# Two delta-rule scans in lockstep, link by link, in shared PSUM tiles

## The chip, the cores and the metric

The kernel runs on one core of a Trainium2 chip. The metric is device time in microseconds. TensorE is called PE here (PEld is its weight load), VectorE DVE, ScalarE ACT, GpSimd POOL and SyncE SP.

## The reference

One inference step of a hybrid diffusion backbone, two layers over 640 tokens (512 latent tokens of a sample and 128 of a prompt), model width 1024. Each layer mixes tokens with three groups of heads side by side, gated DeltaNet (gdn, four heads of 64), HGRN2 (hgrn, four heads of 64) and latent attention (mla), and then runs a SwiGLU feed-forward. The part that matters here is the recurrence of gated DeltaNet, over chunks of 64 tokens, forward and backward:

```python
def step(s, xs):
    att_i, u_i, w_i, qd_i, kt_i, gl_i = xs
    v_new = u_i - jnp.einsum('bhck,bhkv->bhcv', w_i, s)
    o = jnp.einsum('bhck,bhkv->bhcv', qd_i, s) + jnp.einsum('bhij,bhjv->bhiv', att_i, v_new)
    s = s * gl_i[..., None, None] + jnp.einsum('bhck,bhcv->bhkv', kt_i, v_new)
    return s, o
...
s_fin, o = lax.scan(step, s0.astype(F32), xs)
```

HGRN2's recurrence is chunked too; within a chunk its attention matrix is built from pairwise decays.

## The kernel before, in words

All 640 tokens are processed together: activations lie as (128 features, 640 tokens). The large projections (`gemm`, matmuls on line L656) take each weight block of 128x512 from memory, split it into two reduced-precision parts (`wh` on ACT, L632, and `wl` on DVE, L633) and multiply by the two parts of the activation, each matmul 128x128 by 128x320. These matmuls fill most of PE's time.

The heads of gdn form two pairs (pr 0 and 1), a pair lying on the 128 partitions. For a pair, `gdn_raw` makes queries, keys and values from the projection, and `gdn_main` makes the matrices of every chunk: decays, the triangular matrix P, its inverse R (the 16x16 blocks are inverted on DVE by 15 rounds of L866 and L868, with a DMA trip through memory before and after; then transposes from L885, and matmuls from L896 to L921), and at its end it runs the scan. The scan has ten links: eight of the sample and two of the prompt, which alternate at first. A link handles a forward and a backward chunk: ks = K S (four 64x64 fp32 matmuls, L946), r = v - g ks (two DVE operations, L949), xx = R r (four matmuls, L954), vt and VN (two DVE operations, L957 and L958), ds = K^T vt (four matmuls, L964), and the new state S (two DVE operations, L969). Every step needs the one before.

`mix_out` (L985) forms the pair's output afterwards. `hgrn_main` does the same for a pair of hgrn heads: a prelude of exponentials and logarithms over (128, 2, 640) from Abs (L1012) on, then six levels of `merge` (matmuls on L1040, 64x64, with masked copies on L1044), each level needing products on DVE (L1076) and copies on ACT (L1065) between them, and then state matmuls (L1089). `mla_proj` (matmuls on L1208 and L1209) and the attention (from L1276) follow.

What runs beside what comes from a list, one entry a group of chains that take turns, `|` between chains, `+` within a chain, `*2` two turns at a time:

```python
ORDER = "g0 g1 i0|2*e0 i1+L0|2*m0+e1 P0|f0 a0|m1+f1"
```

g is gdn (raw and main), e gdn's output, i hgrn's projection, m hgrn_main, f hgrn's output, L and P the projections of mla, a the attention; the digit is the pair. The program is written in that order, and the framework's scheduler then orders each engine's instructions with a cost model, by priority and program order, and places them as data and buffers allow. So an instruction that waits for data is passed by later ones, such as the large matmuls of the next projection. `use` sets the pools from which blocks and PSUM tiles are taken: a pair's blocks come from `w0` or `w1` (seven buffers each), its small PSUM tiles from `c0` or `c1`. g0, e0, m0 use `w0`; g1, e1, m1 use `w1`, and m0 takes blocks that gdn's pair 0 leaves.

Of the kernel before, what the change touches and what calls it, by code (L numbers as in the profile page):

```python
# [12 lines left out]
ALU = mybir.AluOpType  # L13
# [8 lines left out]
NC = NT // 64  # L22
# [15 lines left out]
HP = (slice(0, 64), slice(64, 128))  # L38
# [121 lines left out]
def two(ap, i0, i1):  # L160
    st = i1 - i0
    if st > 0:
        return ap[:, i0:i1 + 1:st]
    return ap[:, i0:(i1 - 1 if i1 > 0 else None):st]


class Builder:
# [634 lines left out]
    def gdn_main(self, l, pr, KQ, VT):  # L802
        nc = self.nc
        u0 = pr * 2
        flat = lambda ap: ap.rearrange("p d c t -> p (d c t)")
        beta, btail, egl, ngc, g = (ap[:, u0:u0 + 2] for ap in (self.beta, self.btail, self.egl, self.ngc, self.g))
# [6 lines left out]
        for gi in range(3):  # L813
            for which, dst in ((0, E), (1, EG)):
                t = self.ps()
                for i, gu in enumerate(gU):
                    st, sp = i == 0, i == 1
                    if gi < 2:
                        r = gu[:, gi, 0:NCS].rearrange("p c t -> p (c t)")
# [3 lines left out]
                if gi == 2 and which == 0:  # L823
                    for d in range(2):
                        for i, gu in enumerate(gU):
                            nc.tensor.matmul(t[:, d * 128:d * 128 + 128], lhsT=self.LmR[:, d],
                                             rhs=gu[:, d, NCS:].rearrange("p c t -> p (c t)"), start=i == 0, stop=i == 1)
# [4 lines left out]
        for c0 in range(0, NC, 4):  # L832
            n = min(4, NC - c0)
# [8 lines left out]
        att = E  # L842
# [3 lines left out]
        for gp in range(8):  # L846
            b = gp % 4
            nc.sync.dma_start(out=drP[gp].rearrange("u j i -> j u i"),
                              in_=P[gp * 16:gp * 16 + 16].rearrange("p d c t -> p (d c) t")[:, :, b * 16:b * 16 + 16])
# [13 lines left out]
        for j in range(15):  # L863
# [3 lines left out]
                                    in1=W[:, :, j:j + 1, 0:j + 1].to_broadcast(sh), op=ALU.mult)  # L867
# [3 lines left out]
        for gp in range(8):  # L871
            b = gp % 4
            nc.sync.dma_start(out=X[gp * 16:gp * 16 + 16].rearrange("p d c t -> p (d c) t")[:, :, b * 16:b * 16 + 16],
                              in_=drT[gp].rearrange("u j i -> j u i"))
        nc.vector.tensor_tensor(out=EG, in0=EG, in1=KQ[:, 1].unsqueeze(1).to_broadcast([128, 2, NC, 64]), op=ALU.mult)
        K_, V = KQ[:, 1], VT[:, 0].rearrange("p (c t) -> p c t", t=64)
        self.token_major([lambda i: KQ[:, 0, 2 * i:2 * i + 2].rearrange("p c t -> p (c t)"), lambda i: VT[:, 0, i * 128:i * 128 + 128]], [K_, V])
        QD = EG
# [26 lines left out]
        R = self.blk([128, 2, NC, 64])  # L905
# [21 lines left out]
        SH = self.blk([128, 2, NC, 64])  # L927
        VN = self.blk([128, 2, NC, 64])
        fl = lambda ap: ap.rearrange("p d c t -> p (d c) t")
        SHf, VNf = fl(SH), fl(VN)  # L930
        bf = beta.rearrange("p d c -> p (d c)")
        bt = btail.rearrange("p d c -> p (d c)")
        bc2 = lambda ap: ap.unsqueeze(2).to_broadcast([128, 2, 64])
        nc.sync.dma_start(out=two(SHf, 0, NC + NCS - 1), in_=self.I["gst"][l, :, :, pr])
        nc.vector.memset(two(SHf, NCS, 2 * NC - 1), 0.0)
        for step in range(NCS):
            for c0, n in ((0, NCS), (NCS, NC - NCS)):
                if step >= n:
                    continue
                cs = (c0 + step, c0 + n - 1 - step)  # L940
                i0, i1 = cs[0], NC + cs[1]
                last = step == n - 1
                ks = self.ps((128, 2, 64))
                for d in range(2):
                    for h in HP:
                        nc.tensor.matmul(ks[h, d], lhsT=KQ[h, 0, cs[d]], rhs=SH[h, d, cs[d]], start=True, stop=True)  # L946
                r = self.small(f"st_r{pr}", [128, 2, 64], bufs=1)
                for d in range(2):
                    nc.vector.scalar_tensor_tensor(out=r[:, d], in0=ks[:, d], scalar=ngc[:, d, cs[d]:cs[d] + 1], in1=V[:, cs[d]],  # L949
                                                   op0=ALU.mult, op1=ALU.add)  # L950
                xx = self.ps((128, 2, 64))
                for d in range(2):
                    for h in HP:
                        nc.tensor.matmul(xx[h, d], lhsT=R[h, d, cs[d]], rhs=r[h, d], start=True, stop=True)  # L954
                if not (last and c0 == 0):
                    vt = self.small(f"st_v{pr}", [128, 2, 64], bufs=1)
                    nc.vector.tensor_tensor(out=vt, in0=xx, in1=bc2(two(bt, i0, i1)), op=ALU.mult)  # L957
                nc.vector.tensor_tensor(out=two(VNf, i0, i1), in0=xx, in1=bc2(two(bf, i0, i1)), op=ALU.mult)  # L958
                if last and c0 == 0:
                    continue  # L960
                ds = self.ps((128, 2, 64))
                for d in range(2):
                    for h in HP:
                        nc.tensor.matmul(ds[h, d], lhsT=K_[h, cs[d]], rhs=vt[h, d], start=True, stop=True)  # L964
                if last:
                    sto = self.small("stout", [128, 2, 64], bufs=2)
                for d in range(2):
                    dst = sto[:, d] if last else SH[:, d, cs[d] + 1 - 2 * d]
                    nc.vector.scalar_tensor_tensor(out=dst, in0=SH[:, d, cs[d]], scalar=egl[:, d, cs[d]:cs[d] + 1],  # L969
                                                   in1=ds[:, d], op0=ALU.mult, op1=ALU.add)  # L970
                if last:
                    nc.sync.dma_start(out=self.O["gst"][l, :, :, pr], in_=sto)
        return lambda h, c: [(SH[h, d, c], QD[h, d, c]) for d in range(2)] + [(VN[h, d, c], att[h, d, c]) for d in range(2)]

    def mix_out(self, dst, terms):
        nc = self.nc
# [394 lines left out]
    def layer(self, l, h, pre):  # L1371
        nc, I = self.nc, self.I
# [13 lines left out]
                pass  # L1386
        self.use("c0", "w0")
        self.gates(l, inp(W_AB))
        terms, gd, mix, st, mb = [None] * 4, [None] * 2, [None] * 8, [None, None], []

        def gdn(pr):
            self.use(f"c{pr}", f"w{pr}")
            gd[pr] = (rb([128, 2, NC, 64]), rb([128, 2, NT]))
            self.gdn_raw(l, pr, inp, *gd[pr])
            if pr == 0:
                fill(100)
            terms[pr] = self.gdn_main(l, pr, *gd[pr])

        def gdn_end(pr):
            self.use(f"c{pr}", f"w{pr}")  # L1400
# [28 lines left out]
        def hgrn_end(pr):  # L1429
            self.use(f"c{pr}", f"w{pr}")  # L1430
            yield from self.mix_out(hs[pr][0][:, 0], terms[2 + pr])
            mix[2 + pr] = self.finish_mixer(hs[pr][0][:, 0], hs[pr][2], self.vec[:, l, V_HNW:V_HNW + 1], f"w{pr}")

        steps = {"g": gdn, "e": gdn_end, "i": hgrn_in, "m": hgrn, "f": hgrn_end, "L": lambda n: mla_in(), "P": lambda n: mla(),
                 "a": lambda n: self.attention(l, st[1], mix, range(4))}
        for group in ORDER.split():
# [5 lines left out]
        for s in range(2):  # L1442
            tag, bt = f"c{s}", ("w1", "r")[s]
# [24 lines left out]
        last, us = None, []  # L1468
        for i, n in enumerate(range(NSP, NFF)):
# [3 lines left out]
            last = self.seven(l, n, A, us[-1], last, rb([128, 4, HALF]))  # L1473
# [14 lines left out]
        for pieces, ns in (((0, 1), range(4)),) + tuple(((q,), range(4, KD)) for q in (0, 1)):  # L1488
# [13 lines left out]
            tag, bt = f"c{s}", ("h", "w0")[s]  # L1502
# [121 lines left out]
```

## Time and profile before

| | us |
|---|---|
| three runs | 1975.47, 1977.1, 1982.02; median 1977.1 |
| the profiled execution | 1979.4 |
| its span (first to last instruction) | 1977.6 |
| PE busy | 1910.7 (97%) |
| DVE busy | 1370.9 (69%) |
| ACT busy | 997.1 (50%) |
| mean granted PE clock | 0.99 of full |

A row of the profile's groups reads: line, engine, operation, output<-inputs, shapes, count, busy time, mean time of one. Times in the text are microseconds from the span's start. The two layers lie one behind the other; in layer 0 the gdn scans run from 220 to 321, in layer 1 from 1195 to 1300.

### The profile page before, as it was taken

What the parts mean: (1) busy time and instruction counts of PE and PEld (TensorE: products, weight loads), DVE (VectorE), ACT (ScalarE), POOL (GpSimd) and SP (SyncE); (2) the same over time, 40 slices, a digit from 0 to 9 for tenths busy, and PEclk for the clock granted to TensorE, in tenths of its full rate; (3) what the DMA queues carried; (4) which work ended last, traced back from release to release, by engine and by line L of the source; (5) the groups of instructions that cost most, each with busy time, mean ns of one, the idle gap of its engine ahead of it and who ended that gap; (6) DMA issues with size and microseconds to landing.
All of it is one profiled execution on the core that took longest, in us unless ns stands there. A gap on an engine that the chain in (4) does not pass through costs nothing. (4 is left out here: it accounts for less than half of the span.)

```text
span 1977.6 us, 40034 instructions
## 1 busy us (share of the span) xinstructions
PE 1910.7 (97%) x15688; PEld 1739.2 (88%) x15688; DVE 1370.9 (69%) x2962; ACT 997.1 (50%) x2086; POOL 16.2 (1%) x64
## 2 busy tenths in 40 slices
PE   6999999999999999999999999999999999999996
PEld 3748888888999979999998987888899999999996
DVE  5537567696677757788887786678756977776245
ACT  4515253754676435551355551648457755555243
POOL 0000000000000000000000000000000000000000
PEclk9999999999999999999999999999999999999998
DMA  9652211210554452256764232112036532223344
GB/s 320 207 183 64 59 42 28 58 37 18 187 176 150 139 166 85 86 167 202 235 192 133 62 100 52 29 42 58 5 100 187 167 117 86 86 86 103 87 139 141
DMA packets 157486, 226.56 MB, mean 115 GB/s; under 512 B 38769, under 2 KB 65521, under 8 KB 157297
## 3 DMA queue, kind: packets, MB, share of 16 engines
q1 hardware_dynamic: 156656, 222.70, 36.8%
q8 instruction: 123, 2.02, 0.4%
q0 software_dynamic: 640, 1.31, 0.3%
q14 instruction: 67, 0.54, 0.1%
HBM read 209.99 MB, written 12.65 MB: 113 GB/s over the span
## 5 line engine op out<-in xcount | busy, mean ns | idle before, releaser
L632 ACT ACTIVATE wh<-raw 128x512 fp32r<-128x512 f32 (+2 forms) x634 | 391.0, 617 | 603.8 <-PE g L656 413.5
L633 DVE TENSOR_TENSOR wl<-raw,wh 128x512 fp32r<-128x512 f32 (+1 forms) x610 | 408.2, 671 | 303.4 <-ACT wh L632 265.9
L656 PE MATMUL g<-h,wh 128*128 128x320 f32 x2448 | 541.4, 319 | 8.6 <-ACT h L481 3.3
L656 PEld LDWEIGHTS g<-h,wh 128*128 128x128 f32 x2448 | 401.3, 189 | 41.0 <-issue 16.2
L656 PE MATMUL g<-h,wl 128*128 128x320 f32 x1224 | 338.3, 316 | 0.5 <-DVE wl L633 0.5
L656 PE MATMUL g<-w,wh 128*128 128x320 f32 x1152 | 246.1, 314 | 5.5 <-ACT r L1448 5.5
L656 PEld LDWEIGHTS g<-h,wl 128*128 128x128 f32 x1224 | 218.4, 189 | 12.0 <-issue 6.4
L656 PEld LDWEIGHTS g<-w,wh 128*128 128x128 f32 x1152 | 191.0, 191 | 6.2 <-ACT r L1448 6.0
L656 PE MATMUL g<-r,wh 128*128 128x320 f32 x768 | 165.5, 313 | 0.0
L656 PE MATMUL g<-w,wl 128*128 128x320 f32 x480 | 132.7, 314 | 0.0
L563 PE MATMUL g<-h,wh 128*128 128x320 f32 x768 | 129.0, 310 | 0.0
L656 PEld LDWEIGHTS g<-r,wh 128*128 128x128 f32 x768 | 127.5, 190 | 0.6
L563 PEld LDWEIGHTS g<-h,wh 128*128 128x128 f32 x768 | 116.3, 188 | 3.6 <-issue 3.4
L557 DVE TENSOR_TENSOR raw<-raw,raw 128x512 f32<-128x512 f32 x128 | 88.0, 687 | 2.2
L656 PEld LDWEIGHTS g<-w,wl 128*128 128x128 f32 x480 | 87.4, 192 | 0.2
L563 PE MATMUL g<-w,wh 128*128 128x320 f32 x512 | 85.9, 310 | 0.0
L563 PE MATMUL g<-r,wh 128*128 128x320 f32 x512 | 85.5, 309 | 0.0
L299 DVE SCALAR_TENSOR_TENSOR h<-h,silu_c,h 128x512 f32<-128x512 f32 x112 | 78.5, 745 | 4.6 <-DMA h<-in_w_ada_dram 4.5
L563 PEld LDWEIGHTS g<-w,wh 128*128 128x128 f32 x512 | 77.6, 188 | 3.4 <-ACT r L575 3.4
L656 PE MATMUL g<-r,wl 128*128 128x320 f32 x288 | 79.3, 312 | 0.0
L563 PEld LDWEIGHTS g<-r,wh 128*128 128x128 f32 x512 | 77.7, 188 | 0.0
L563 PE MATMUL g<-h,wl 128*128 128x320 f32 x384 | 71.9, 309 | 0.0
(378 smaller groups left out, 3094.8 us busy)
## 6 DMA issues: line engine op xcount, KB each, us to landing
raw<-in_w_ffi_dram SPq DMA_DIRECT2D x224, 256.0 KB
raw<-in_w_ffo_dram SPq DMA_DIRECT2D x120, 256.0 KB
raw<-in_w_in_dram SPq DMA_DIRECT2D x106, 256.0 KB
w<-in_w_ada_dram SPq DMA_DIRECT2D x96, 256.0 KB
raw<-in_w_out_dram SPq DMA_DIRECT2D x64, 256.0 KB
h<-in_w_ada_dram SPq DMA_DIRECT2D x32, 512.0 KB
r<-in_w_ada_dram SPq DMA_DIRECT2D x32, 256.0 KB
r<-in_xT_dram SPq DMA_DIRECT2D x6, 640.0 KB
```

The source lines that it names most:

```text
L299: nc.vector.scalar_tensor_tensor(out=acc[:, s], in0=raw[:, k % 2], scalar=c, in1=acc[:, s], op0=ALU.mult, op1=ALU.add)
L557: nc.vector.tensor_tensor(out=o, in0=a, in1=b, op=ALU.add)
L563: nc.tensor.matmul(ps, lhsT=w[e][:, k], rhs=a[f][:, k], start=first and i == 0, stop=i == 11, skip_group_check=not first)
L632: self.nc.scalar.activation(hi, src, AF.Copy)
L633: self.nc.vector.tensor_tensor(out=lo, in0=src, in1=hi.bitcast(F32), op=ALU.subtract)
L656: self.nc.tensor.matmul(ps[h], lhsT=w[:, k], rhs=rhs(e, kk, h), start=(kk == 0 and i == 0), stop=(kk == nk - 1 and i == 2))
```

## The change

The scan becomes a generator that yields after each of its steps. `gdn_main` returns it instead of running it, and a new function, `gdn_scan`, runs after the matrices of pair 1 are made, and goes through the ten links with both pairs: ks of pair 0 and of pair 1, then r of both, and so on. For each link the two pairs share three PSUM tiles, (128, 2, 2, 64) instead of (128, 2, 64), with one half for each pair, and two small tiles, `st_r` and `st_v`. The number of instructions and their shapes stay. In the changed kernel the scan's lines are L944, L947, L952, L955, L960, L961 and L969, and lines from L985 on lie 12 lower (L985 is L997, L1040 is L1052, L1208 is L1220).

```diff
+        def scan(step, c0, n, both):
...
+            ks, xx, ds = (both[i][:, pr] for i in range(3))
+            r, vt = (both[i][:, pr] for i in (3, 4))
+            for d in range(2):
+                for h in HP:
+                    nc.tensor.matmul(ks[h, d], lhsT=KQ[h, 0, cs[d]], rhs=SH[h, d, cs[d]], start=True, stop=True)
+            yield
...
+        return scan, lambda h, c: [(SH[h, d, c], QD[h, d, c]) for d in range(2)] + [(VN[h, d, c], att[h, d, c]) for d in range(2)]
+
+    def gdn_scan(self, scans):
         for step in range(NCS):
             for c0, n in ((0, NCS), (NCS, NC - NCS)):
                 if step >= n:
                     continue
...
-                ks = self.ps((128, 2, 64))
...
-                r = self.small(f"st_r{pr}", [128, 2, 64], bufs=1)
...
-        return lambda h, c: [(SH[h, d, c], QD[h, d, c]) for d in range(2)] + [(VN[h, d, c], att[h, d, c]) for d in range(2)]
+                both = [self.ps((128, 2, 2, 64), tag) for tag in ("c0", "c1", "c0")]
+                both += [self.small(name, [128, 2, 2, 64], bufs=1) for name in ("st_r", "st_v")]
+                runs = [scan(step, c0, n, both) for scan in scans]
+                while runs:
+                    runs = [r for r in runs if next(r, runs) is not runs]
...
         def gdn(pr):
...
-            terms[pr] = self.gdn_main(l, pr, *gd[pr])
+            scans[pr], terms[pr] = self.gdn_main(l, pr, *gd[pr])
+            if pr == 1:
+                self.gdn_scan(scans)
```

The order of the instructions follows from the scheduler. On DVE, in layer 0, pair 1's block inversion (L866, L868) stands like this before, with the links of pair 0's scan between its rounds (`st_r` and `st_v` are the scan's small tiles, `w` blocks, `m` PSUM tiles):

```order
L866 TENSOR_TENSOR w_258_1893<-w_258_1893,w_257_1892 80x2x48
L868 TENSOR_TENSOR w_257_1892<-w_257_1892,w_258_1893 80x2x12x4
L969 SCALAR_TENSOR_TENSOR w_148_1269<-w_148_1269,eg_592,m_1312 128x64 x2
...
L949 SCALAR_TENSOR_TENSOR st_r_161_1324<-m_1319,eg_592,r_603 128x64 x2
L866 TENSOR_TENSOR w_258_1893<-w_258_1893,w_257_1892 80x2x55
L868 TENSOR_TENSOR w_257_1892<-w_257_1892,w_258_1893 80x2x11x5
L957 TENSOR_TENSOR st_v_163_1332<-m_1327,eg_592 128x128
L958 TENSOR_TENSOR w_149_1270<-m_1327,beta_575 128x2x64
```

and like this after:

```order
L866 TENSOR_TENSOR w_209_1670<-w_209_1670,w_208_1669 80x2x48
L868 TENSOR_TENSOR w_208_1669<-w_208_1669,w_209_1670 80x2x12x4
L866 TENSOR_TENSOR w_209_1670<-w_209_1670,w_208_1669 80x2x55
L868 TENSOR_TENSOR w_208_1669<-w_208_1669,w_209_1670 80x2x11x5
L866 TENSOR_TENSOR w_209_1670<-w_209_1670,w_208_1669 80x2x60
L868 TENSOR_TENSOR w_208_1669<-w_208_1669,w_209_1670 80x2x10x6
```

The scan's operations have moved behind the inversion; on PE, 194 large matmuls (213 in layer 1) stand beside it with only pair 0's first ks ahead of them. On PE, in layer 1, the scan's last third is a run without large matmuls after the change (`r` and `w` are the scan's operands; 66 matmuls in all stand in it):

```order
L960 MATMUL m_13404<-st_v_13406,r_11892 64x64 x4
L960 MATMUL m_13404<-st_v_13406,r_12522 64x64 x4
L944 MATMUL m_13443<-w_1836_12518,r_11892 64x64 x4
L944 MATMUL m_13443<-w_1912_13148,r_12522 64x64 x4
L952 MATMUL m_13444<-st_r_13446,w_1833_12428 64x64 x4
L952 MATMUL m_13444<-st_r_13446,w_1909_13058 64x64 x4
L960 MATMUL m_13445<-st_v_13447,r_11892 64x64 x4
L960 MATMUL m_13445<-st_v_13447,r_12522 64x64 x4
L944 MATMUL m_13484<-w_1836_12518,r_11892 64x64 x4
L944 MATMUL m_13484<-w_1912_13148,r_12522 64x64 x4
```

Before, a link of either pair had large matmuls or merges of m0 between its steps to its end. The merges of m0 stood, in layer 1, on PE like this before (L1040, with scan 1 and large matmuls, `g`, between them):

```order
L1040 MATMUL m_14066<-r_11621,w_2118_14035 64x64
L1040 MATMUL m_14084<-r_11621,w_2118_14035 64x64 x4
L656 MATMUL g_14777<-h_11046,wh_14810 128x320
L656 MATMUL g_14778<-h_11560,wh_14810 128x320
L656 MATMUL g_14777<-h_11048,wh_14810 128x320
L946 MATMUL m_13538<-w_2007_13417,r_12791 64x64 x4
L656 MATMUL g_14778<-h_11562,wh_14810 128x320
...
L964 MATMUL m_13554<-st_v_2038_13551,r_12791 64x64 x4
L656 MATMUL g_14778<-h_11562,wh_14810 128x320
L656 MATMUL g_14777<-h_11046,wl_14811 128x320
L1040 MATMUL m_14161<-w_2112_14006,w_2118_14035 64x64 x3
```

and like this after (L1052; L754 are transposes, L1125 matmuls of a norm):

```order
L1125 MATMUL m_14979<-w_2138_14973,cst 128x320
L1052 MATMUL m_13974<-r_11575,w_2026_13943 64x64 x16
L1052 MATMUL m_13992<-r_11575,w_2026_13943 64x64 x4
L754 MATMUL m_15528<-cst,r_13846 128x128 x4
L754 MATMUL m_15537<-cst,r_13846 128x128
L1052 MATMUL m_14069<-w_2020_13914,w_2026_13943 64x64 x16
L1052 MATMUL m_14087<-w_2020_13914,w_2026_13943 64x64 x4
L1052 MATMUL m_14100<-w_2020_13914,w_2026_13943 64x64 x16
L1052 MATMUL m_14118<-w_2020_13914,w_2026_13943 64x64 x4
L1052 MATMUL m_14195<-w_2020_13914,w_2026_13943 64x64 x16
```

In both layers the merges now stand in one run without large matmuls. Between the last matmul of the scans and the first merge stand 92 large matmuls in layer 0 and 47 in layer 1, with the output matmuls of both pairs. Over the whole program the places where a stretch of large matmuls is broken by other matmuls went from 234 to 219. Outside the stretch from g1 to the attention of each layer PE's order is as before.

## Rows read from the trace of the kernel before

**Rows 1.** The page: busy time, share of the span, instructions.

```profile
PE 1910.7 (97%) x15688; PEld 1739.2 (88%) x15688; DVE 1370.9 (69%) x2962; ACT 997.1 (50%) x2086; POOL 16.2 (1%) x64
```

**Rows 2.** Windows: stretch and length, busy time by engine (instructions), granted clock, DMA.

```profile
220.60:260.00 39.40, 39.37 (x370) 30.85 (x372) 24.36 (x94) 7.00 (x15) 0.00 (x0) 1.00 0.18 49
...
367.40:412.80 45.40, 42.96 (x340) 36.97 (x339) 37.92 (x67) 38.76 (x77) 2.17 (x4) 1.00 0.25 65
...
1256.60:1301.80 45.20, 43.93 (x540) 36.38 (x541) 33.66 (x100) 20.92 (x43) 0.00 (x0) 1.00 0.11 31
...
1331.20:1375.00 43.80, 41.53 (x329) 35.49 (x329) 36.57 (x63) 37.13 (x75) 2.04 (x4) 1.00 0.25 67
```

**Rows 3.** Windows of line L656 alone: PE, PEld.

```profile
220.60:260.00 39.40, 30.10 (x144) 21.46 (x144) 1.00 0.18 49
...
1140.00:1150.00 10.00, 9.16 (x63) 8.93 (x62) 1.00 0.34 98
```

**Rows 4.** Timeline of PE: start, time, engine, line, records.

```profile
254.35 0.45 PE L946 MATMUL m<-w,r 64*64 64x64 f32 x8
254.73 0.56 PE L656 MATMUL g<-h,wl 128*128 128x320 f32 x2
255.13 0.45 PE L656 MATMUL g<-h,wh 128*128 128x320 f32 x2
255.52 0.45 PE L954 MATMUL m<-st_r,w 64*64 64x64 f32 x8
```

**Rows 5.** Timeline of PE in layer 1: a run of merges and one alone.

```profile
1301.92 1.27 PE L1040 MATMUL m<-w,w 64*64 64x64 f32 x38
...
1303.04 0.22 PE L1040 MATMUL m<-w,w 64*64 64x64 f32 x1
```

**Rows 6.** Timeline of DVE: block inversions and the transposes behind them.

```profile
174.22 0.19 DVE L866 TENSOR_TENSOR w<-w,w 80x30 f32<-80x30 f32 x1
...
190.69 0.18 DVE L868 TENSOR_TENSOR w<-w,w 80x30 f32<-80x30 f32 x1
...
206.10 1.51 DVE L885 STREAM_TRANSPOSE w<-w 128x1280 f32<-128x1280 f32 x1
...
219.15 0.19 DVE L866 TENSOR_TENSOR w<-w,w 80x30 f32<-80x30 f32 x1
...
248.83 0.18 DVE L868 TENSOR_TENSOR w<-w,w 80x30 f32<-80x30 f32 x1
...
261.90 1.51 DVE L885 STREAM_TRANSPOSE w<-w 128x1280 f32<-128x1280 f32 x1 [1.19 <-DMA w<-drT]
```

**Rows 7.** Timeline: a ds step and the state update behind it.

```profile
229.41 0.45 PE L964 MATMUL m<-st_v,r 64*64 64x64 f32 x8
...
229.91 0.47 DVE L969 SCALAR_TENSOR_TENSOR w<-w,eg,m 128x64 f32<-128x64 f32 x2 [0.22 <-PE m L964]
```

**Rows 8.** Windows of line L1040 alone: PE, PEld, in pair 1's scans.

```profile
279.00:324.30 45.30, 9.43 (x200) 8.21 (x200) 1.00 0.10 30
...
1256.60:1301.80 45.20, 7.84 (x160) 6.86 (x160) 1.00 0.11 31
```

**Rows 9.** Groups of 1277 to 1311, by form: m0's levels.

```profile
L1076 DVE TENSOR_TENSOR w<-w,w 128x320 f32<-128x320 f32 x18 | 8.3, 483 | 0.1
L1065 ACT ACTIVATE w<-w 128x320 f32<-128x320 f32 x10 | 4.6, 476 | 17.2 <-DVE w L1076 15.4 <-PE m L1040 1.8
L1044 DVE COPY_PREDICATED w<-cst,m 128x512 f32<-128x512 uint32 x6 | 4.4, 731 | 0.1
```

**Rows 10.** Timeline: m0's first operation and its first merge in layer 0.

```profile
273.39 1.26 ACT L1012 ACTIVATE w<-r 128x1280 f32<-128x1280 f32 x1
...
294.36 0.45 PE L1040 MATMUL m<-w,w 64*64 64x64 f32 x5
```

**Rows 11.** Groups of ACT, 273 to 295.

```profile
L407 ACT ACTIVATE w<-w 128x1280 f32<-128x1280 f32 x2 | 2.5, 1272 | 0.4 <-DVE w L1015 0.3
```

**Rows 12.** Windows, columns as in rows 2.

```profile
546.80:550.20 3.40, 1.01 (x7) 1.01 (x8) 2.62 (x4) 3.02 (x6) 0.00 (x0) 1.00 0.53 141
550.20:553.60 3.40, 3.40 (x14) 3.40 (x14) 1.85 (x4) 1.10 (x2) 0.00 (x0) 0.50 0.91 290
```

More of the change, by code (lines that the diff above doesn't have):

```diff
@@ L935, in gdn_main @@
         nc.vector.memset(two(SHf, NCS, 2 * NC - 1), 0.0)
+        def scan(step, c0, n, both):
+            cs = (c0 + step, c0 + n - 1 - step)
+            i0, i1 = cs[0], NC + cs[1]
+            last = step == n - 1
+            ks, xx, ds = (both[i][:, pr] for i in range(3))
[4 more added lines that the diff above has]
+            yield
+            for d in range(2):
+                nc.vector.scalar_tensor_tensor(out=r[:, d], in0=ks[:, d], scalar=ngc[:, d, cs[d]:cs[d] + 1], in1=V[:, cs[d]],
+                                               op0=ALU.mult, op1=ALU.add)
+            yield
+            for d in range(2):
+                for h in HP:
+                    nc.tensor.matmul(xx[h, d], lhsT=R[h, d, cs[d]], rhs=r[h, d], start=True, stop=True)
+            yield
+            if not (last and c0 == 0):
+                nc.vector.tensor_tensor(out=vt, in0=xx, in1=bc2(two(bt, i0, i1)), op=ALU.mult)
+            yield
+            if not (last and c0 == 0):
+                for d in range(2):
+                    for h in HP:
+                        nc.tensor.matmul(ds[h, d], lhsT=K_[h, cs[d]], rhs=vt[h, d], start=True, stop=True)
+            nc.vector.tensor_tensor(out=two(VNf, i0, i1), in0=xx, in1=bc2(two(bf, i0, i1)), op=ALU.mult)
+            yield
+            if last and c0 == 0:
+                return
+            if last:
+                sto = self.small("stout", [128, 2, 64], bufs=2)
+            for d in range(2):
+                dst = sto[:, d] if last else SH[:, d, cs[d] + 1 - 2 * d]
+                nc.vector.scalar_tensor_tensor(out=dst, in0=SH[:, d, cs[d]], scalar=egl[:, d, cs[d]:cs[d] + 1],
+                                               in1=ds[:, d], op0=ALU.mult, op1=ALU.add)
+            if last:
+                nc.sync.dma_start(out=self.O["gst"][l, :, :, pr], in_=sto)
+        return scan, lambda h, c: [(SH[h, d, c], QD[h, d, c]) for d in range(2)] + [(VN[h, d, c], att[h, d, c]) for d in range(2)]
+    def gdn_scan(self, scans):
         for step in range(NCS):
@@ L939, in gdn_main @@
                     continue
-                cs = (c0 + step, c0 + n - 1 - step)
-                i0, i1 = cs[0], NC + cs[1]
-                last = step == n - 1
-                ks = self.ps((128, 2, 64))
-                for d in range(2):
-                    for h in HP:
-                        nc.tensor.matmul(ks[h, d], lhsT=KQ[h, 0, cs[d]], rhs=SH[h, d, cs[d]], start=True, stop=True)
-                r = self.small(f"st_r{pr}", [128, 2, 64], bufs=1)
-                for d in range(2):
-                    nc.vector.scalar_tensor_tensor(out=r[:, d], in0=ks[:, d], scalar=ngc[:, d, cs[d]:cs[d] + 1], in1=V[:, cs[d]],
-                                                   op0=ALU.mult, op1=ALU.add)
@@ L951, in gdn_main @@
[L951 to L970, printed above, removed]
@@ L971, in gdn_main @@
-                if last:
-                    nc.sync.dma_start(out=self.O["gst"][l, :, :, pr], in_=sto)
-        return lambda h, c: [(SH[h, d, c], QD[h, d, c]) for d in range(2)] + [(VN[h, d, c], att[h, d, c]) for d in range(2)]
+                both = [self.ps((128, 2, 2, 64), tag) for tag in ("c0", "c1", "c0")]
[3 more added lines that the diff above has]
+                    runs = [r for r in runs if next(r, runs) is not runs]
@@ L1388, in layer @@
         self.gates(l, inp(W_AB))
+        scans = [None] * 2
         terms, gd, mix, st, mb = [None] * 4, [None] * 2, [None] * 8, [None, None], []
```

## The prediction

> **What bounds the kernel now.** I read the page's busy shares first: TensorE (PE) works 97% of the span [rows 1], so time can come only from work that PE no longer does or from idle that it does not have now. Then I read the stages that the change touches, window by window. In pair 0's scan of layer 0 PE is busy 39.37 of 39.40 us, in pair 1's scan of layer 1 43.93 of 45.20, and only the stage of P0, behind the hgrn chain m0, shows idle: 45.40 - 42.96 = 2.4 us in layer 0 and 43.80 - 41.53 = 2.3 us in layer 1 [rows 2]. The granted clock is 1.00 in all of them. So the scan, a serial chain, costs almost no waiting today, because the projection's large matmuls (L656) lie between its links: 144 of them in pair 0's scan window [rows 3]. A large matmul costs 9.16 / 63 = 0.145 us in a stretch without scan work [rows 3].
>
> A scan fragment in that stream costs more than its matmuls. (One of these fp32 matmuls leaves two records, so a hop of one pair, four matmuls, shows as eight.) From the eight records of ks at 254.35 to the eight of xx at 255.52 there are four large matmuls, so 1.17 us hold 0.58 us of large matmuls and 0.59 us of one such fragment [rows 4]. In a long run, small matmuls follow one another at (1.27 - 0.22) / 37 = 0.028 us (38 records in 1.27 us, a single one lasting about 0.22 [rows 5]), so eight would need 0.22 us, and 0.37 us is the price of breaking the stream.
>
> **The change, part by part.**
>
> *Sharing.* No instruction is added or removed. The matmuls of two pairs lie nearer together, so the large-matmul stream is broken in 219 places of the program order instead of 234: 15 x 0.37 = **-5.5 us** (bounds 0 and -5.5). The price is that VectorE's first operation on a shared tile waits for both pairs' matmuls, and that a hop carries two pairs' VectorE work.
>
> *A bare block in g1.* Scan 0 leaves g1, and 194 large matmuls (213 in layer 1) stand with no scan work ahead of pair 1's inverse (L896). They last 194 x 0.145 = 28 us and end near 220.6 + 28 = 248.7. Pair 1's inverse must be there by then. Its VectorE chain L866/L868 starts at 219.15; it took 29.7 us beside scan 0, but pair 0's own, with no scan beside it, took 174.22 to 190.69, 16.5 us. The DMA trip behind it, to L885, took 15.4 us for pair 0 (190.69 to 206.10) and 13.1 us for pair 1 (248.83 to 261.90) [rows 6]. So L885 starts at 219.15 + 16.5 + 13.1 to 15.4 = 248.7 to 251.0, and with its own 1.51 us and some 0.9 us of copies the inverse can begin at 251 to 253.5: 2.5 to 5 us after PE has nothing left. Against it, SP issues those DMAs behind weight loads that wait for buffers, and a bare block empties these faster; so the lower end is 0. I take +2 a layer, **+4 us** (0 to +14; layer 1, where only the order was read, is taken like layer 0, with a higher upper end).
>
> *The scan's tail in layer 1.* The filler ends before the scan: 66 scan matmuls follow one another, about eight hops of ds, ks and xx. A hop is, from rows: 0.50 us from the ds matmuls' start to the state update (229.41 to 229.91) and 0.47 us for two updates [rows 7]; I take vt's hop for the same. With the second pair's operations on the same engine it is 0.97 us (they overlap the next hop) to 0.50 + 2 x 0.47 = 1.44 us, so eight take 7.8 to 11.5 us, less their own 8 x 16 x 0.028 = 3.6 us of matmul time: **+6 us** (+4 to +8). In layer 0 the filler lasts to the end: 0.
>
> *hgrn's chain m0 without filler.* Today 200 of layer 0's and 160 of layer 1's 280 merge records lie inside pair 1's scan window [rows 8], among large matmuls. After the change they follow one another in both layers, with only a few transposes and norm matmuls between. A level of the merge needs, by rows: 40 records on PE (1.1 us), four VectorE products of 0.483 (pipelined some 0.42), ScalarE's copies of 0.476, and the masked copies of 0.731 and, for the prompt's chunks, an estimated 0.3 on VectorE [rows 9]. VectorE alone then needs 4 x 0.42 + 1.03 + some 0.3 for the decays' product = 3.0 us a level, 18 us for six; PE has 280 x 0.028 = 7.8 us in them, and 1 to 2 us of transposes and norms. Uncovered: 18 - 9.5 = 8.5. If only the chain merge, two products, merge counts (2.4 us a level) it is 14.4 - 9.5 = 5. I take 7 a layer, **+14 us** (+10 to +22).
>
> *hgrn's prelude.* m0 cannot begin before pair 0's blocks are free, that is after the lockstep scan and pair 0's output matmuls. From its Abs (L1012, 273.39) to its first merge (294.36) took 21.0 us beside scan 1 [rows 10]. By the code eight passes over 128x1280 stand one behind the other, of the size of Abs (1.26) and of the two L407 (1.27 each), 10.3 us, and three VectorE operations that I put at 0.8 us each from their size: about 13 us [rows 10, 11]. PE's cover for it in the new order is 92 large matmuls in layer 0 (13.3 us) and 47 in layer 1 (6.8 us), with some 4 us of small matmuls in both: 17 and 11 us. Uncovered: 0 to 4 us and 2 to 10 us, more if ScalarE is late. I take 3 + 7 = **+10 us** (+2 to +20).
>
> *What is given back.* The 4.7 us of idle in P0's stages [rows 2] came from weights split late on ScalarE and VectorE; with these engines freed by a waiting PE I take **-3 us** (0 to -4.7).
>
> The sum is -5.5 + 4 + 6 + 14 + 10 - 3 = **+25.5 us** on the profiled execution's 1979.4 us (span 1977.6), 2004.9 us. The runs' median is 1977.1, 2.3 us below that execution, so I predict 2003 us.
>
> **The clock.** After a stretch in which PE was busy 1.01 of 3.40 us, the next stretch shows the granted clock 0.50 (1.2 GHz) and 14 records [rows 12], where 3.40 / 0.145 = 23 large ones would fit: some 9 x 0.145 = 1.3 us lost. One or two such drops, behind the prelude's waits, lie within the range. The Trainium skill, TensorE: Matmul & The Clock Gate, section "Why this matters for your kernels", advises against idle gaps of TensorE in mid-kernel because the clock falls after them; these two rows agree with it. It speaks against this change, which makes such gaps where there are none.
>
> **The rivals.**
>
> *Faster.* The filler that g1 uses up is not missed: m0's chain and prelude run fast enough on emptier engines, and P0's stall goes. Then -5.5 - 4.7 gives 1967 us. For it: VectorE is busy only 24.36 and 33.66 us in the two scan windows [rows 2], and the small matmuls need little of PE. Against it: the merges' VectorE need of 18 us against 9.5 us of PE work is a sum of measured durations. It decides if all uncovered waits together stay under about 4 us. Chance 0.09.
>
> *No change.* Waits of 4 to 16 us in all, as when the merge chain is 2.4 us a level, the prelude is hidden by its cover and g1's block ends with pair 1's chain, make up for what is saved: 1977 us. Chance 0.11.
>
> *The clock falls in the merge chain.* PE is busy 9.5 of 18 us in it, between the 30% that went ahead of the drop in [rows 12] and full work. At half the clock its small matmuls take up to 7.8 us more a layer, 15 us in both: 2018 us. For it: prelude and chain follow one another, both with gaps. Against it: VectorE sets the pace in the chain, so that part of the slower PE work is hidden. Chance 0.18.
>
> **How the numbers follow.** The likeliest case, with 0.62, is slower by uncovered waits: 2003 us, in its own range 1987 to 2016 us (+10, with most terms near their low ends: -5.5 - 4.7 + 0 + 4 + 10 + 6, to 13 us above the sum). Runs of this kernel can tell about 0.3%, 6 us, from no change. Faster 0.09, same 0.11, slower 0.62 + 0.18 = 0.80. The range goes from 1976, where the rival without change lies mostly inside, to 2026, which holds the clock's price and leaves out only several terms at their upper ends together.
>
> **What would show it.** In the profile after, PE's busy time should fall by a few us while the span grows. Layer 0's and layer 1's stages from the lockstep scan's end to the first U matmuls (L1220) should show PE idle of 5 to 20 us each, ended by VectorE's products (L1088, today L1076) and the prelude's operations; the merges should lie in one run of about 18 us. In layer 1 the last third of the scan should show PE waiting for L947, L955 and L969 in turn. Before pair 1's inverse, PE should wait 0 to 5 us for DMA and VectorE. P0's stage should be a little shorter. I am wrong if the large matmuls of g1 turn out slower than 0.145 us, because weights then bound that block, if m0's merges keep PE full, or if the waits all show but fall where PE had been waiting anyway.

## The result, and the profile after

The changed kernel takes 2031.53 us (median of four runs, 2030.6 to 2033.44) against 1979.56 us before: 1.0256 times as long, with a 95% interval of 1.024 to 1.0272, or 52 us more. The forecast was slower, 2003 us, with a range that ended at 2026 us.

The page of the changed kernel: PE has the same instructions, and is busy 20.6 us longer than in [rows 1].

```profile
PE 1931.3 (95%) x15688; PEld 1758.2 (87%) x15688; DVE 1372.4 (68%) x2962; ACT 1000.1 (49%) x2086; POOL 16.2 (1%) x64
```

The stages of the changed kernel, by windows of PE alone (stretch and length, busy time, granted clock, DMA). In each layer they are: from pair 0's first ks to pair 1's inverse; the inverse; the lockstep scan; from there to the first U matmul (both outputs, hgrn's prelude and merges); and on to the first attention matmul.

```profile
223.50:252.50 29.00, 29.00 (x204) 1.00 0.29 76
252.50:261.50 9.00, 9.00 (x263) 1.00 0.24 69
261.50:318.00 56.50, 55.72 (x606) 1.00 0.08 25
318.00:384.20 66.20, 52.83 (x786) 0.89 0.09 29
384.20:434.40 50.20, 48.35 (x367) 0.94 0.22 60
1219.50:1251.30 31.80, 31.80 (x222) 1.00 0.29 75
1251.30:1260.50 9.20, 9.08 (x264) 1.00 0.14 39
1260.50:1313.00 52.50, 48.70 (x585) 0.95 0.10 27
1313.00:1380.80 67.80, 49.59 (x717) 0.78 0.07 19
1380.80:1429.80 49.00, 49.00 (x389) 0.94 0.22 62
```

The same view of the kernel before, from pair 0's first ks to the first attention matmul of each layer: scan 0, inverse, scan 1, the rest to U, and P0's stage.

```profile
220.60:269.30 48.70, 48.67 (x551) 1.00 0.17 42
269.30:279.00 9.70, 9.40 (x270) 1.00 0.12 35
279.00:321.00 42.00, 41.62 (x561) 1.00 0.10 30
321.00:367.40 46.40, 46.40 (x523) 1.00 0.19 55
367.40:412.20 44.80, 42.36 (x336) 1.00 0.25 66
1195.50:1246.80 51.30, 51.30 (x569) 1.00 0.18 46
1246.80:1256.60 9.80, 9.43 (x270) 1.00 0.09 25
1256.60:1300.80 44.20, 42.93 (x526) 1.00 0.11 31
1300.80:1331.20 30.40, 30.28 (x459) 1.00 0.18 51
1331.20:1375.00 43.80, 41.53 (x329) 1.00 0.25 67
```

The reader adds up each block. Layer 0 takes 210.9 instead of 191.6 us, layer 1 210.3 instead of 179.5: 50.1 us, nearly the whole loss. Idle time of PE grows from 3.1 to 16.0 us in layer 0 and from 4.0 to 22.1 in layer 1, 31.0 us together. The other 19.1 us are PE busy longer with the same work, and the clock column points to the reason: before it is 1.00 in every stage, after it is 0.78 to 0.95 in five of them. A mean of 0.78 over 67.8 us, between the two levels 1.0 and 0.5, is 67.8 x 0.22 x 2 = 30 us at half clock; all five make about 61 us. In these 61 us PE is busy 44.7 us. By the merges below, which take 1.38 us at the upper level and 2.40 at the lower, the same work would take 25.7 us at the upper one, 19 us less (an estimate).

Where the pace of hgrn's merges comes from is seen in a timeline of layer 0 of the changed kernel (L1052 merges, L1056 masked copies, L1088 products):

```profile
361.25 1.38 PE L1052 MATMUL m<-w,w 64*64 64x64 f32 x40 [1.39 <-DVE w L1088]
...
364.51 1.38 PE L1052 MATMUL m<-w,w 64*64 64x64 f32 x40 [1.88 <-DVE w L1088]
...
367.76 2.40 PE L1052 MATMUL m<-w,w 64*64 64x64 f32 x40 [1.87 <-DVE w L1088]
...
369.77 0.90 DVE L1056 COPY_PREDICATED w<-cst,m 128x512 f32<-128x512 uint32 x2 [0.75 <-PE m L1052]
370.58 1.69 DVE L1088 TENSOR_TENSOR w<-w,w 128x320 f32<-128x320 f32 x4
371.61 2.40 PE L1052 MATMUL m<-w,w 64*64 64x64 f32 x40 [1.45 <-DVE w L1088]
```

A level takes 3.26 and 3.25 us at first (361.25, 364.51, 367.76). Then the same 40 records take 2.40 in place of 1.38 us, and a level 3.85 us (367.76 to 371.61). What PE did ahead of the fall is in the same rows: it waited 1.4 to 1.9 us of each level. The copy waits for the merges, the products stand behind the copy on VectorE, and the next merges wait for the products: the work of two engines in one chain, with nothing else on PE. Of the 14 runs of merges that m0 has in the two layers, two in layer 0 and five in layer 1 take 2.40 us.

### The profile page after: what moved, and what is told of

Same layout as the page of the kernel before. It is cut to its first block, busy times and chain, and to the rows that moved or that the text cites. A ratio compares the mean times of both kernels' runs of the same rounds, so it can differ in the third digit from the quotient of the medians.

```text
span 2031.7 us, 40030 instructions
## 1 busy us (share of the span) xinstructions
PE 1931.3 (95%) x15688; PEld 1758.2 (87%) x15688; DVE 1372.4 (68%) x2962; ACT 1000.1 (49%) x2086; POOL 16.2 (1%) x64
## 4 chain that ended last, share of the span: by engine, by line
PE 83%; DVE 7%; ACT 5%; DMA 2%; issue 2%; SPq 0%; DVEq 0%; ACTq 0%
PE g L656 41%; PE g L563 19%; PE m L319 3%; PE m L997 2%; PE m L1052 2%; PE m L1330 2%; DVE wl L633 1%; DMA h<-in_w_ada_dram 1%; DVE h L299 1%; PE m L354 1%; PE g L1237 1%; PE m L952 1%; PE g L1220 1%; PE m L279 1%; PE m L944 1%
## 5 line engine op out<-in xcount | busy, mean ns | idle before, releaser
L633 DVE TENSOR_TENSOR wl<-raw,wh 128x512 fp32r<-128x512 f32 (+1 forms) x610 | 408.7, 672 | 337.3 <-ACT wh L632 305.1
L656 PE MATMUL g<-h,wh 128*128 128x320 f32 x2448 | 532.7, 318 | 8.1 <-ACT h L481 3.3
L656 PEld LDWEIGHTS g<-h,wh 128*128 128x128 f32 x2448 | 401.2, 190 | 38.9 <-issue 17.0
L656 PE MATMUL g<-h,wl 128*128 128x320 f32 x1224 | 336.3, 316 | 0.8 <-DVE wl L633 0.5
L656 PE MATMUL g<-w,wh 128*128 128x320 f32 x1152 | 246.0, 314 | 5.5 <-ACT r L1463 5.5
L656 PEld LDWEIGHTS g<-h,wl 128*128 128x128 f32 x1224 | 218.6, 189 | 12.0 <-issue 7.0
L656 PEld LDWEIGHTS g<-w,wh 128*128 128x128 f32 x1152 | 191.5, 191 | 6.2 <-ACT r L1463 6.0
L656 PE MATMUL g<-r,wh 128*128 128x320 f32 x768 | 165.1, 312 | 0.0
L656 PE MATMUL g<-w,wl 128*128 128x320 f32 x480 | 132.5, 314 | 0.0
L563 PE MATMUL g<-h,wh 128*128 128x320 f32 x768 | 129.1, 310 | 0.0
L656 PEld LDWEIGHTS g<-r,wh 128*128 128x128 f32 x768 | 126.9, 189 | 0.6
L656 PEld LDWEIGHTS g<-w,wl 128*128 128x128 f32 x480 | 87.4, 192 | 0.2
L656 PE MATMUL g<-r,wl 128*128 128x320 f32 x288 | 79.3, 311 | 0.0
```

The costliest lines, as they stand in the source:

```text
L563: nc.tensor.matmul(ps, lhsT=w[e][:, k], rhs=a[f][:, k], start=first and i == 0, stop=i == 11, skip_group_check=not first)
L633: self.nc.vector.tensor_tensor(out=lo, in0=src, in1=hi.bitcast(F32), op=ALU.subtract)
L656: self.nc.tensor.matmul(ps[h], lhsT=w[:, k], rhs=rhs(e, kk, h), start=(kk == 0 and i == 0), stop=(kk == nk - 1 and i == 2))
```

## Experiments

All times are medians; each kernel was compared with the kernel before on the same chip.

**Own tiles for each pair.** The lockstep stays in the program, only the sharing goes:

```diff
-            ks, xx, ds = (both[i][:, pr] for i in range(3))
-            r, vt = (both[i][:, pr] for i in (3, 4))
+            ks, xx, ds, r, vt = both
...
-                both = [self.ps((128, 2, 2, 64), tag) for tag in ("c0", "c1", "c0")]
-                both += [self.small(name, [128, 2, 2, 64], bufs=1) for name in ("st_r", "st_v")]
-                runs = [scan(step, c0, n, both) for scan in scans]
+                runs = []
+                for pr, scan in enumerate(scans):
+                    both = [self.ps((128, 2, 64), f"c{pr}") for i in range(3)]
+                    both += [self.small(f"{name}{pr}", [128, 2, 64], bufs=1) for name in ("st_r", "st_v")]
+                    runs.append(scan(step, c0, n, both))
```

> Lockstep in the program as in the change, but each pair keeps its own PSUM and small tiles. If the shared tiles are what ties pair 0's scan to pair 1's matrices (theory), the scheduler is free to run scan 0 beside g1's large matmuls again, m0 starts early, and the time is that of before: 1975 to 1990 us. If the place in the program or the lockstep order itself costs (rival), it stays near the changed kernel: 2025 to 2035 us.

Measured: 1979.99 us, ratio to before 0.9995 (0.9985 to 1.0004). The whole loss is gone although the program is still written link by link. In the order of its instructions scan 0 lies again among g1's large matmuls (78 of its 80 ks records beside 163 large ones, 224.7 to 268.5): the scheduler does not keep to the order of the program, but to what is ready, and only a tile that both pairs write holds pair 0 back. The lockstep order by itself costs nothing that can be measured, although m0 still starts later than before: its first merge in layer 0 comes 91 us after pair 0's first ks, against 74 before and 126 in the change.

**Which of the two kinds of tile.** First the PSUM tiles shared and the small tiles apart, then the other way round:

```diff
-            r, vt = (both[i][:, pr] for i in (3, 4))
+            r, vt = both[3 + pr], both[5 + pr]
...
```

> Lockstep with shared PSUM tiles and each pair's own small tiles. Its order on PE is that of the change. Theory (either kind of sharing alone ties the pairs): 2027 to 2035 us. Rival, that st_r and st_v are what ties them on the chip: 1980 to 2005 us.

```diff
-            ks, xx, ds = (both[i][:, pr] for i in range(3))
-            r, vt = (both[i][:, pr] for i in (3, 4))
+            ks, xx, ds = both[2 + pr]
+            r, vt = (both[i][:, pr] for i in (0, 1))
...
```

> Lockstep with shared small tiles and each pair's own PSUM tiles. By its order pair 0 stops one step later than in the change (after its first ks and xx matmuls), the scan is in more fragments, and in layer 0 some large matmuls stay for m0's merges. Theory: tied as well, 2020 to 2040 us. Rival, that PSUM sharing alone is what costs: 1980 to 2000 us.

Measured: 2030.71 us (ratio 1.0262, 1.0238 to 1.0286) and 2025.03 us (1.023, 1.0206 to 1.0254). Either kind alone ties the pairs.

**Layer 1 alone.** In layer 0 `gdn_scan` is called for each pair by itself, at the end of its own `gdn`.

```diff
...
-            if pr == 1:
+            if l in ALONE:
+                self.gdn_scan([scans[pr]])
+            elif pr == 1:
                 self.gdn_scan(scans)
```

> Lockstep in shared tiles in layer 1 alone; in layer 0 each scan runs where it ran before. By the stages of the two traces (from pair 0's first ks to the first attention matmul) the change costs 19 us in layer 0 and 31 us in layer 1. Theory, that each layer's loss is made in that stretch and is not given back or carried on: 2007 to 2015 us. Rival, that part of the loss lies elsewhere (weight prefetch or clock of later stages): under 2003 or over 2020 us.

Measured: 2009.34 us, 29.6 us above before (ratio 1.015, 1.0129 to 1.0171). By the windows layer 1's stretch had grown by 30.8 us. The loss is made in each layer's stretch and not given back later.

**hgrn's prelude early.** Two blocks of their own let the prelude of m0 run during the scans. They need room, so its control has 11 blocks instead of 12 in `r` and 4 raw weight buffers instead of 7.

```diff
-BUFS = {"h": 8, "r": 12, "w0": 7, "w1": 7}
-NRAW = 7
+BUFS = {"h": 8, "r": 11, "w0": 7, "w1": 7, "x": 2}
+NRAW = 4
...
-        QP = self.blk([128, 2, NT])
-        KS = self.blk([128, 2, NT])
+        QP, KS = qk or [self.blk([128, 2, NT]) for _ in range(2)]
...
         def hgrn_in(pr):
+            if pr == 0:
+                qk.extend(self.blk([128, 2, NT], tag="x") for _ in range(2))
```

> The change with 11 instead of 12 blocks in the pool r and 4 instead of 7 raw weight buffers, as the control of the next kernel. By its order the large matmuls of mla's input come later: layer 1's lockstep scan then has none between its steps (26 hops in a row), and half of m0's merges have some. Theory of uncovered waits: 26 hops of about 1.4 us, less 0.45 us of matmuls, minus some 10 us gained in m0: 2035 to 2050 us. Rival, that m0's chain alone is what costs: 2010 to 2025 us.

> The control with two blocks of their own for m0's prelude, so that its exponentials run during the scans and m0's first merge follows pair 0's output at once. Theory, that the prelude's wait and the bare merges cost 10 to 20 us a layer: 15 to 35 us below the control. Rival, that the lockstep scan sets the end by itself: within 5 us of the control.

Measured: 2034.89 us for the control (ratio 1.0273, 1.0247 to 1.0299) and 2002.89 us with the early prelude (1.0107, 1.0075 to 1.0138): 32 us less. Windows of PE, from pair 0's first ks to the first attention matmul, layer 0 and layer 1, for the control:

```profile
222.20:434.40 212.20, 197.24 (x2215) 0.92 0.16 43
1228.40:1429.30 200.90, 178.72 (x2139) 0.92 0.15 42
```

and with the early prelude:

```profile
221.00:416.00 195.00, 189.68 (x2250) 0.96 0.17 47
1214.20:1401.20 187.00, 175.74 (x2170) 0.91 0.16 45
```

The two stretches are 31.1 us shorter: 20.6 us less idle time of PE (16.6 instead of 37.1) and 10.5 us less busy time. m0's first merge comes some 15 us earlier in each. More than half of the loss thus hung on the late start of m0, behind the scan that was held back. On the kernel before, the same two blocks give nothing (last experiment). The control came out just below the range that the theory gave it, and from its level nothing follows: the smaller buffers alone cost the kernel before some 10 to 13 us (below). Only the difference of the two counts.

**Fillers against the clock.** Matmuls whose result nothing reads, behind each merge level of m0, three and then two of them:

```diff
+            if pr == 0:
+                for _ in range(NDUM):
+                    nc.tensor.matmul(self.ps((128, HALF)), lhsT=self.onesD, rhs=KM[:, 0:HALF], start=True, stop=True)
```

> The change, with up to three fp32 matmuls 128x128 by 128x320 (about 0.55 us each) added behind each merge level of m0 (pair 0 only); their results are read by nothing. Theory, that the merge chain leaves PE half idle, that the clock falls for it, and that a slower PE lengthens the chain: the granted clock stays near 1.00 in the merges, a level falls from 3.87 to about 3.25 us, the matmuls behind it run at full clock too: 2010 to 2028 us although PE has 18 to 20 us more work. Rival, that the lower clock is hidden because VectorE sets the pace: the added work lies in idle time at best, 2031 to 2050 us.

> As the kernel with fillers, with two in place of three behind each merge level of m0, whose results nothing reads. With three a level took 3.82 us at full clock, since the merges waited for the fillers' 1.88 us. Theory: two (1.25 us) fit behind the masked copy, the clock holds, a level takes about 3.25 us as in the change at full clock: 2020 to 2027 us, below the change with some 20 us more matmul work. Rival: the clock does not hold with two or the levels do not shorten, 2029 to 2036 us.

Measured: 2030.18 us (ratio 1.0244, 1.0225 to 1.0263) with three, 2028.64 us (1.0243, 1.022 to 1.0266) with two; both intervals overlap that of the change. With two, the timeline of PE and VectorE in layer 1 (L1084 fillers, L1053 merges, L1057 copies) reads:

```profile
1362.40 1.38 PE L1053 MATMUL m<-w,w 64*64 64x64 f32 x40
...
1363.76 0.91 DVE L1057 COPY_PREDICATED w<-cst,m 128x512 f32<-128x512 uint32 x2
1364.54 1.34 PE L1084 MATMUL m<-w,onesD 128*128 128x320 f32 x4 [0.75 <-DVE w L1057]
...
1365.81 1.38 PE L1053 MATMUL m<-w,w 64*64 64x64 f32 x40
```

The merges are back at 1.38 us and a level takes 3.41 us, not 3.85 as in the rows of the changed kernel; a level with more work in it is shorter. But with 48 records of fillers added (4 in 1.34 us, so 16 us) the whole kernel comes out 3 us lower, which the intervals don't separate from nothing. What the clock costs inside the merges is small: the 0.4 us of a level, for the seven levels that the change has at the lower clock, make 3 us.

The next kernel added fillers in the last third of layer 1's scan and in its prelude too.

```diff
+    def idle_fill(self, x, n):
+        for _ in range(n):
+            self.nc.tensor.matmul(self.ps((128, x.shape[1])), lhsT=self.onesD, rhs=x, start=True, stop=True)
...
+                if l == 1 and step > 3:
+                    self.idle_fill(vt.rearrange("p d t -> p (d t)"), 2)
...
+        if l == 1 and pr == 0:
+            self.idle_fill(QP[:, 0, 0:HALF], 5)
```

> The change with two fillers behind each merge level of m0, and in layer 1 also fillers in the last third of the scan and in m0's prelude, each bound by its input to its place; no result of them is read. Theory, that about a third of the 52 us is a slower PE and not waiting: the granted clock stays near 1.00 in layer 1 until the merges end, where the change has 30 us of half clock, and the time is 2012 to 2024 us. Rival, that the half clock in these places is hidden behind waits: 2025 us or more, since the fillers themselves stand in the way of the scan and the merges.

Measured: 2037.5 us (ratio 1.0289, 1.0271 to 1.0308). Windows of PE in layer 1, from the lockstep scan's start to its last ks and from there to U:

```profile
1251.90:1308.00 56.10, 53.46 (x614) 1.00 0.08 25
1308.00:1382.90 74.90, 62.67 (x794) 0.90 0.06 17
```

The same of the change:

```profile
1260.50:1310.10 49.60, 45.80 (x556) 0.98 0.11 28
1310.10:1380.80 70.70, 52.49 (x746) 0.77 0.06 18
```

The clock rose from 0.77 to 0.90, and both stretches became longer. The fillers stand in the way of the links: from the ds matmuls to the next ks it is 3.6 us (1297.83 to 1301.41) where the change takes 1.07. m0's prelude, from Abs to the first merge, takes 21.2 us instead of 19.5; that the fillers cause this was not tested. So these runs don't tell how much of the 52 us a full clock would give back; that it is a third is not borne out.

**Masked copies behind the products.** If the products only stand behind the copy on VectorE, changing places should shorten a level.

```diff
             for s in range(2):
                 for dst, d in ((KS[:, s], s), (QP[:, s], 1 - s)):
...
+            for a, c, t, mask in later:
+                nc.vector.copy_predicated(att[:, a:c], mask.unsqueeze(1).to_broadcast([128, c - a, 64]).bitcast(U32), t)
```

> The change with the masked copies of hgrn's merges written behind the same level's products, so that VectorE does the products first. Theory, that in the change a level is one chain (merges, masked copy, products, merges: 3.25 us at full clock, 3.87 at half), because the products stand behind the copy on VectorE: a level falls by up to the copies' 0.9 us, to 2.4 to 3.0 us at full clock, over about ten bare levels 4 to 9 us: 2022 to 2028 us. Rival, that VectorE's sum of about 3.0 us a level sets the pace whatever the order: 2028 to 2034 us.

Measured: 2034.15 us (ratio 1.0275, 1.0251 to 1.0299), no gain. In layer 1 a level (L1091 products, L1093 copies) is now:

```profile
1361.56 2.40 PE L1052 MATMUL m<-w,w 64*64 64x64 f32 x40 [1.72 <-DVE w L1093]
...
1363.99 0.89 DVE L1091 TENSOR_TENSOR w<-w,w 128x320 f32<-128x320 f32 x2 [0.87 <-PE m L1052]
1364.80 0.90 DVE L1093 COPY_PREDICATED w<-cst,m 128x512 f32<-128x512 uint32 x2
1365.61 0.89 DVE L1091 TENSOR_TENSOR w<-w,w 128x320 f32<-128x320 f32 x2
1365.67 2.40 PE L1052 MATMUL m<-w,w 64*64 64x64 f32 x40 [1.71 <-DVE w L1093]
```

It takes 4.11 us (1361.56 to 1365.67) instead of 3.85. The next merges now wait for the copy itself: a merge uses both PSUM buffers of `c0`, one for the sample's chunks and one for the prompt's, and these come free only when the copy has read them. My theory was half wrong: the chain is as I read it, but the copy is in it whichever way VectorE takes the two.

**A version that beats both?** The early prelude was tried on the kernel before, with its own control:

> The kernel before with 11 blocks in the pool r and 4 raw weight buffers in place of 12 and 7, as the control of the next one. Its order on PE in the mixer is that of before; fewer raw buffers can delay weights: 1977 to 1995 us.

> The control of before with two blocks of their own for m0's prelude. m0 then merges from pair 1's scan on, about 10 us earlier, and U can start before m1 takes ScalarE. Theory, that what m0's start is bound to sets PE's idle in P0's stage (2.4 us a layer): 2 to 6 us below its control. Rival, that this idle is ScalarE's load and not m0's start: within 2 us of the control.

Measured: 1992.42 us for the control (ratio 1.0052, 1.0035 to 1.0069) and 1989.74 us (1.0044, 1.0024 to 1.0063). The smaller buffers cost 0.5%, the early prelude gives nothing that can be told from its control, although m0's first merge comes 15 and 23 us earlier in the two stretches: where m0 is hidden already, starting it earlier is worth nothing here. No kernel of this study beats the one before.

## Why the prediction was off

The direction and the waits as a mechanism were right; the size was short by half, and the range ended 5.5 us short of it. What the forecast lacked is a slower PE: it priced the clock at almost nothing. Step by step, with idle time of PE from the windows above:

- **A bare block in g1 (+4).** Measured 0: PE is busy 29.00 of 29.00 and 31.80 of 31.80 us there. The rows of the changed kernel that answer to [rows 6]:

```profile
221.49 0.19 DVE L866 TENSOR_TENSOR w<-w,w 80x30 f32<-80x30 f32 x1
...
235.56 0.19 DVE L868 TENSOR_TENSOR w<-w,w 80x30 f32<-80x30 f32 x1
...
248.10 1.51 DVE L885 STREAM_TRANSPOSE w<-w 128x1280 f32<-128x1280 f32 x1
```

 The block inversion takes 14.1 us (16.5 forecast) and the DMA trip 12.5 us (13.1 to 15.4 forecast), so the inverse begins 4.4 us later, at 252.49, just as the large matmuls run out.

- **The scan's tail in layer 1 (+6).** Idle time in the inverse and scan stages went from 0.7 to 0.8 us in layer 0 and from 1.6 to 3.9 us in layer 1: +2.4 us. Hops are as long as forecast, 1.07 and 1.29 us, but the wait in each is short:

```profile
1300.43 0.68 PE L960 MATMUL m<-st_v,r 64*64 64x64 f32 x16 [0.52 <-DVE st_v L955]
1301.50 0.91 PE L944 MATMUL m<-w,r 64*64 64x64 f32 x16 [0.39 <-DVE w L969]
1302.79 0.91 PE L952 MATMUL m<-st_r,w 64*64 64x64 f32 x16 [0.39 <-DVE st_r L947]
```

 PE counts as busy to the end of the last record, 0.7 to 0.9 us a hop, while I took off 0.45 us for it.

- **m0's chain (+14) and prelude (+10).** The stage that holds both went from 0.1 us of idle to 13.4 + 18.2: +31.5 us against +24. The longest waits of PE in it, in layer 0 and then in layer 1 (total, times, longest):

```profile
PE m L1052 <- DVE w L1088: 6.6, 4, 1.9
PE g L1221 <- ACT r L632: 3.6, 1, 3.6
...
PE m L1052 <- DVE w L1088: 6.4, 4, 2.0
PE m L1125 <- ACT w L1122: 5.4, 1, 5.4
```

 The merges' waits for VectorE make 15.8 us in both layers (6.6, 6.4, and 2.8 where a masked copy stood behind other VectorE work), near the +14: a level was put at 3.0 us and took 3.07 to 3.26 at full clock in layer 0. The waits between the prelude's Abs and the first merge make 6.2 us (5.4 and 0.8), less than the +10, although this takes 17.2 and 19.5 us, not 13. Some 9.5 us lie behind the merges, before the transposes, state matmuls and U, where the forecast had no term.

- **Given back in P0 (-3).** 4.7 us of idle became 1.9: -2.9 us. What PE waited for there before was not the weights' split, as the forecast read it, but mostly that of the activations (L633 into blocks, 1.1 and 0.7 of layer 0's 2.4 us).

- **All waits.** 31.5 + 2.4 - 2.9 is 31.0 us; the terms of the forecast that are waits (4 + 6 + 14 + 10 - 3) also make 31. That the sums agree is luck: two terms were 7.6 us too high, the stage of m0 7.5 us too low.

- **Sharing (-5.5) and the clock.** Here is the step that failed. The forecast let PE's busy time fall by 5.5 us; in the two stretches it rose by 19.1. The saving by sharing is not what was missing: the large matmuls (L656, 1076 in both kernels) are busy 190.7 us in the two stretches instead of 202.8. These 12 us can't be set against the rest one to one, since records overlap. What failed is the price of the clock, and with it PE's busy time. The paragraph on it put "one or two such drops" at 1.3 us each and took them as part of the range; the trace has about 61 us at half clock. The rival in which the clock falls in the merge chain had 0.18 and its own 15 us. It is nearest to what happened, but it too was too small, since it looked at the merges alone: half clock also lies on layer 1's last links and the output matmuls behind them (0.95 over 52.5 us), on the transposes behind the merges, and on U and what follows it (0.94 over about 50 us in each layer). Against that rival stood that VectorE sets the pace in the chain, so that part of the slower PE work is hidden. That held in part: 1.38 us of merges turned to 2.40, 1.02 more, and a level grew by 0.60, since the copy waits for the merges.

The price of a fragment was not tested by itself. In layer 0's lockstep scan, at clock 1.00, 158 large matmuls (22.9 us at 0.145) and some 440 records of the scan (12.3 us at 0.028) would fill 35 of 55.7 busy us. Most of the rest must lie at the breaks between them, but what one break costs, and what 15 fewer saved, no run separates.

The Trainium skill, TensorE: Matmul & The Clock Gate, section "Why this matters for your kernels", warned of idle gaps in mid-kernel. The trace agrees: the stage with 18.2 us of idle has the granted clock 0.78, and the same stage before, with 0.1 us, has 1.00. I had cited it and then priced it by two rows of a short stall [rows 12] rather than for stages of 66 us that wait again and again.

What stays open is the split of the 50 us: idle and busy time are measured, but not what a full clock would have given, since part of the longer matmuls only takes the place of waits. The kernel with shared PSUM tiles gives a hint, because its trace has the same 15688 PE records in the same order as the change. Its two stretches, from pair 0's first ks to the first attention matmul:

```profile
219.50:431.70 212.20, 197.53 (x2215) 0.94 0.16 43
1213.30:1425.80 212.50, 191.28 (x2168) 0.87 0.15 40
```

By the clock column they hold about 81 us at half clock, 20 more than the change, and take 3.5 us longer (424.7 against 421.2): PE is busy 5.7 us longer and idle 2.2 us less. At that rate the 61 us would be worth some 10 of the 50 us. Some 40 us of loss would then be left at full clock, against 25.5 forecast, so the waits would be sized too small as well. That is an estimate from one pair of executions; no run shows it.

## What to carry to other kernels

Under a scheduler that works by readiness, a tile that two independent chains share is a dependence: check what each chain waited for before, and who waits behind it, since what was lost here is not in the scans but in hgrn two stages later. Filler work is a stock: using it in a stage that would otherwise be idle takes it from a later stage, so count it over all stages that need it. When a change opens gaps on a busy TensorE, look for the slower clock in the whole half-idle stage and in the full one behind it, not only in the gaps, and then ask how much of the longer work only fills waits: here fillers brought the clock from 0.77 to 0.90 and gained nothing.

## What the runs showed of the hardware that was not expected

Forty merge records take 1.38 us at the upper clock and 2.40 us at the lower, and a level 3.25 and 3.85 us. Sixteen records of ds (L961) take 0.68 us and, further on in the same scan, where the granted clock is 0.52 (1277 to 1287), 1.12 us, as this timeline of the kernel with lockstep in layer 1 alone shows:

```profile
1275.88 0.68 PE L961 MATMUL m<-st_v,r 64*64 64x64 f32 x16 [0.52 <-DVE st_v L956]
...
1282.91 1.12 PE L953 MATMUL m<-st_r,w 64*64 64x64 f32 x16 [0.39 <-DVE st_r L948]
1284.42 1.12 PE L961 MATMUL m<-st_v,r 64*64 64x64 f32 x16 [0.39 <-DVE st_v L956]
```

PE waits only 0.39 us of a hop of 1.51 us there, and the clock stays at its lower level all the same. Where the clock falls differs from one execution to the next: with the same PE order, the clock fell 1.7 us before the last ks of layer 1's scan in the change (1308.1) and 9.3 us before it in the kernel with shared PSUM tiles (1296.1).
